# A Gram matrix in a linear-attention encoder layer: one fp32 matmul replaced by three float32r passes over split operands

## The chip, the cores and the metric

The kernel runs on one NeuronCore of a Trainium2 chip. Its engines are TensorE (PE in the profile, with PEld for its weight loads), VectorE (DVE), ScalarE (ACT), GpSimd (POOL) and SyncE (SP), which issues most of the DMAs. Each engine takes its instructions from a queue of its own, in order; semaphores join the engines. The metric is the device time of one execution in microseconds: 1487.59 us in the median of three runs of the kernel before (1486.43 to 1488.28).

## What is computed

One encoder layer on 256 tokens of width 2048, all in float32:

```python
h    = rms_norm(x, norm1_g)
proj = h @ w_in                                  # 2048 -> 11312 columns, split among the mixers
y_m  = mlstm_mixer(m_q, m_k, m_v, m_o, ...)      # 4 heads, two directions
y_d  = gated_deltanet_mixer(d_qkv, d_z, ...)     # 8 heads of 128, two directions, chunks of 64
x = x + (sigmoid(g_m) * (y_m @ w_branch_m) + sigmoid(g_d) * (y_d @ w_branch_d)) @ w_out
x = x + relu(rms_norm(x, norm2_g) @ w_ff1) ** 2 @ w_ff2
return rms_norm(x, norm_f_g)
```

In the DeltaNet mixer each head and direction needs, per stretch of tokens, the products of the keys with the keys and of the keys with the queries, weighted by decays, and a triangular solve with the first of them:

```python
a_mat = where(strict, einsum('id,jd->ij', kb, kc) * gamma, 0) + eye(L)
u = triangular_solve(a_mat, vc * beta);  w = triangular_solve(a_mat, kb * exp(gc))
attn = einsum('id,jd->ij', qc, kc) * gamma
```

The two products, keys with keys and keys with queries, are the Gram matrix that the change is about.

## The kernel before

**The weight stream.** Every large product (projection, branch products, output product, the two feed-forward products) is cut into granules of two 128-row tiles of a weight matrix, up to 512 columns each. For a granule SP loads `raw`, ACT rounds it to float32r (`wh`), DVE subtracts to get the rest (`wl`), and PE does three passes: high weights with high activations, low with high, high with low. Four `wh`/`wl` buffers hold granules that are split three ahead of PE. A granule of 512 columns is 12 matmuls; its results collect in PSUM tiles of the pool `ps_acc`, of which there are four, two to a chunk of a product.

**The mixers beside it.** Everything else is written as tasks (Python generators) that yield the engine they want next. A planner (`_Clocks`, `pick`, `pump`, `force`) keeps an estimated clock for each engine from a table of costs (`cost`, L60) and puts a task's next step into the program between two half granules when its estimated inputs are ready. The order that comes out is fixed in the program. `force` (L251) is used where the stream can't go on until some task has moved: it then puts in the tasks' steps one after another, whatever their time. A granule's matmuls, and what is forced while they are asked for, are put in with `clk.quiet` set (L415), under which `issue` (L94) leaves the clocks as they are.

**The DeltaNet task.** `mixers` runs, in this order, `delta_solve(0)` (heads 0 to 3), the mLSTM, `delta_solve(1)` (heads 4 to 7). One `delta_solve` is a long chain: the Gram matmuls of four heads (`pk`, L1036 to L1043, two to a head, each 128 by 512: the 512 columns of `kq` are 256 tokens of keys and 256 of queries), their weighting by decays into `ba` on DVE, a 32 by 32 inversion on DVE of which the inputs and results go through DRAM (`dpx`, `nblk`, `xblk`, `Rb`), small matmuls that widen the inverse (`pz`, `pp`, into `u`), and then a block solve in two steps, each `pA`, `Y`, `pR`, `vy` or `vx`, `pB`, `Y`, and at last the outputs `po`. `delta_out` scales them (`yd`), sums their squares (`jkd`, `ssd`), takes the root (`rs`, `rd`) and multiplies by the gates.

**The shared slots.** The tag `tmp` has four 512-column buffers. The gate product `z` comes in two chunks that hold two each (`sgz`) from their evacuation until `z_mul` (L829) has used them, which needs `so1`, the end of `delta_out` of the second four heads. The evacuation of a chunk of the merge gates `gm` takes two (`sgm`, L1267), and the branch product `bm` of the same number waits for it. A chunk gives its two PSUM accumulators back after its evacuation only; the next chunk asks for two (`mms` in `gemm`):

```python
                    while left["acc"] < 2:
                        force()
```

The tag `w4` has three buffers, used by the convolution, the gates' rows and the inversion.

Of the kernel before, what the change touches and what calls it, by code (L numbers as in the profile page):

```python
# [9 lines left out]
F32 = mybir.dt.float32  # L10
F32R = mybir.dt.float32r
# [5 lines left out]
P = 128  # L17
# [32 lines left out]
class _Clocks:  # L50
# [9 lines left out]
    def cost(self, e, name, a, k):  # L60
        if name == "dma_start":
            return 1.1 if e == "G" else 0.1
        if e == "T":

            sw, self.slab = 0.3 if self.slab else 0.0, False
            if name == "transpose":
                return 0.11 + sw
            n = a[2].free_size()
            c = 4 * max(n, 128) / 2400
            if "tile_position" in k:  # L70
                c *= max(a[1].free_size(), 32) / 128
            return c + sw
        n = a[0].free_size()
        src = a[1] if len(a) > 1 and hasattr(a[1], "free_size") else None
        ps = src is not None and src.space == PSUM
        if e == "A":
            c = ((61 if ps else 112) + n) / 1200
            if any(hasattr(k.get(x), "free_size") for x in ("scale", "bias")):
                c += 0.093
            if "accum_out" in k:  # L80
                c += 0.19
            f = TABLES.get(a[2]) if name == "activation" else None
            if f and f != self.table:
                self.table = f
                c += 1.3
            return c
        if e == "V":
            if name == "reciprocal":
                return 0.1 + 8 * n / 960
            half = name in ("tensor_copy", "tensor_scalar") and not ps and a[0].space != PSUM  # L90
            return (66 + (n / 2 if half else n)) * 1.042e-3 + (0.06 if "scalar" in name else 0)
        return 0.1 + n * (2.2e-3 if name != "memset" else 0.9e-3)
# [64 lines left out]
def layer_kernel(ctx, tc, x, xt, cst, prm, w_in, w_bm, w_bd, w_out, w_ff1, w_ff2, gf, out):  # L157
    nc = tc.nc
    clk = _Clocks()
    V, A, T, G = (_Ordered(tc, e, k, clk) for e, k in  # L160
                  ((nc.vector, "V"), (nc.scalar, "A"), (nc.tensor, "T"), (nc.gpsimd, "G")))
# [112 lines left out]
    def get(what, n, e):  # L274
        while left[what] < n:
            yield None
        left[what] -= n
        yield e

    def put(what, n):  # L280
        left[what] += n

    def psm(shape, name):
        while not psfree:
            yield None
        clk.cur.ext = max(clk.cur.ext, psfree.pop(0))
        yield "T"
        return ps_m.tile(shape, F32, tag="m", name=name)

    def rel(n=1):  # L290
        psfree.extend([clk.cur.last()] * n)
# [144 lines left out]
    pm = mx.enter_context(tc.tile_pool(name="pm", bufs=1))  # L436
# [586 lines left out]
    def delta_solve(grp):  # L1023
# [8 lines left out]
        kq, bd, rq = D[grp]["kq"], D[grp]["bd"], D[grp]["rq"]  # L1032
        ba = pm.tile([P, 4, 2, 768], F32, tag="ba", name="ba")
        bk = ba[:, :, 0, :].rearrange("p h (b c) -> p h b c", c=128)
        clk.cur.fork()
        for hh in range(4):  # L1036
            clk.cur.fork()
            pks = []
            for s_ in range(2):
                pk = yield from psm([P, 2, 256], "pk")  # L1040
                pks.append(pk)
                T.matmul(pk.rearrange("p a b -> p (a b)"), kq[:, hh, s_ * 128:s_ * 128 + 128], kq[:, hh, :],
                         start=True, stop=True)  # L1043
            for s_, pcs in ((0, ((0, 0, 256, 0), (1, 384, 512, 0))), (1, ((0, 256, 384, 128), (1, 512, 768, 0)))):
                yield "V"
                for d, lo, hi, t0 in pcs:
                    n = hi - lo
                    V.scalar_tensor_tensor(ba[:, hh, :, lo:hi], pks[s_][:, :, t0:t0 + n], bd[:, d, s_, hh:hh + 1],
                                           cm[:, hh, lo:hi].unsqueeze(1).broadcast_to([P, 2, n]),
                                           op0=ALU.mult, op1=ALU.mult)  # L1050
                rel()
# [23 lines left out]
        for r in range(31, 0, -1):  # L1075
            n = 32 - r
# [21 lines left out]
        for d in range(2):  # L1098
            for pp in range(2):
# [3 lines left out]
                for hh in range(4):  # L1103
                    for t in range(2):
                        u = unit(d, hh, t)
                        c = DIAG[d, t] + 32 * b1
# [38 lines left out]
        for stp in range(2):  # L1145
# [3 lines left out]
            else:  # L1149
                vts = []  # L1150
                pxs = []
                for d in range(2):
                    px = yield from psm([P, 4, 128], "px")
                    pxs.append(px)
                    c = 128 if d == 0 else 512
                    for hh in range(4):
                        T.matmul(px[:, hh, :], ba[:, hh, 0, c:c + 128], Y[:, d, 1 - tt_[d], hh, :],
                                 start=True, stop=True)
# [20 lines left out]
            for d in range(2):  # L1179
# [3 lines left out]
                for hh in range(4):  # L1183
                    c = DIAG[d, tt_[d]] + hb.start
# [30 lines left out]
        for t in range(2):  # L1215
# [3 lines left out]
            for hh in range(4):  # L1219
                for i, (d, s_, c) in enumerate(lst):  # L1220
                    T.matmul(po[:, hh, :], ba[:, hh, 1, c:c + 128], Y[:, d, s_, hh, :], start=(i == 0),
                             stop=(i == 2))
# [28 lines left out]
    def mixers():  # L1251
        yield from delta_solve(0)
        yield from mlstm_weights()
        yield from mlstm_heads()
        yield from delta_solve(1)
        ydT[0] = pm.tile([P, 16, S], F32R, tag="ba", name="ydT")
        yield from wait_for("T", "z0", "z512")
        yield from y_T(yd[0], ydT[0][:, 0:8, :], ydT[0][:, 8:16, :], lambda kt: dgc)
        done("ydT")
# [528 lines left out]
```

## Time and profile before

| | |
|---|---|
| runs | 1487.59 us median (1486.43 to 1488.28) |
| the profiled execution's own time | 1486.63 us |
| its span, from the first instruction to the last | 1484.8 us |
| mean granted TensorE clock | 0.998 of full |
| PE busy | 1472.0 us, 99% |
| PEld busy | 1235.2 us, 83% |
| DVE busy | 923.9 us, 62% |
| ACT busy | 770.3 us, 52% |
| share of PE in the chain that ended last | 93% |

A matmul's duration in the profile runs from its start to its modelled end, and neighbours overlap, so what a matmul costs is read from start to start. A matmul in fp32 shows as two recorded instructions, one in float32r as one. "x96" in a row of a view that merges neighbours is 96 recorded instructions one after another. Times of the views count from the start of the span.

### The profile page before, as it was taken

How to read it: one execution, taken by the hardware profiler on the slowest of the kernel's cores; microseconds unless marked ns; L12 is line 12 of the kernel's file. 1: busy time of each engine (PE TensorE's matmuls, PEld its weight loads, DVE VectorE, ACT ScalarE, POOL GpSimd, SP SyncE). 2: the span in 40 equal slices, each digit the busy share in tenths (PEclk: the TensorE clock that was granted, in tenths of full speed). 3: DMA queues.
4: the chain of work that ended last, by engine and by line, in shares of the span. 5: the costliest groups of instructions: out<-in, count | busy, mean ns of one | idle time of the engine just before them, and what ended most of it. 6: DMA issues, size and time to landing. Idle time of an engine off the chain costs nothing.

```text
span 1484.8 us, 20192 instructions
## 1 busy us (share of the span) xinstructions
PE 1472.0 (99%) x7604; PEld 1235.2 (83%) x7604; DVE 923.9 (62%) x1400; ACT 770.3 (52%) x1128; POOL 29.2 (2%) x68
## 2 busy tenths in 40 slices
PE   9999999999999999999999999999999999999997
PEld 8787788888878888888888888888888888888886
DVE  6678784378779546565556565555555555555865
ACT  6686545565765456444544444444344444444664
POOL 0000110000010100000000000000000000000000
PEclk9999999999999999999999999999999999999999
DMA  9665576465667845777656666666666666666664
GB/s 317 205 201 169 171 209 187 149 180 160 182 196 225 245 114 150 217 255 252 201 171 199 188 189 190 185 187 189 191 182 189 196 193 193 196 191 194 186 199 140
DMA packets 147730, 287.01 MB, mean 193 GB/s; under 512 B 9956, under 2 KB 24804, under 8 KB 147632
## 3 DMA queue, kind: packets, MB, share of 16 engines
q1 hardware_dynamic: 145088, 278.78, 62.3%
q0 software_dynamic: 2256, 6.58, 1.3%
q8 instruction: 59, 0.97, 0.3%
q10 hardware_dynamic: 288, 0.37, 0.1%
q14 instruction: 39, 0.32, 0.1%
HBM read 278.32 MB, written 7.36 MB: 192 GB/s over the span
## 4 chain that ended last, share of the span: by engine, by line
PE 93%; DMA 3%; ACT 2%; DVE 1%; issue 1%; SPq 0%; ACTq 0%
PE f L125 24%; PE y L125 23%; PE gd L125 6%; PE gm L125 6%; PE wo L125 6%; PE d L125 5%; PE mv L125 3%; PE bd L125 3%; PE bm L125 3%; DMA raw<-in_w_in_dram 3%; PE z L125 2%; PE mq L125 1%; PE mk L125 1%; PE o L125 1%; PE pk L125 1%; ACT wh L125 1%
## 5 line engine op out<-in xcount | busy, mean ns | idle before, releaser
L125 DVE TENSOR_TENSOR wl<-raw,wh 128x1024 fp32r<-128x1024 f32 (+3 forms) x508 | 603.8, 1193 | 468.9 <-ACT wh L125 467.5
L125 ACT CAST wh<-raw 128x1024 fp32r<-128x1024 f32 (+3 forms) x508 | 520.7, 1028 | 562.1 <-PE y L125 162.4
L125 PE MATMUL f<-h,wh 128*128 128x512 f32 x1024 | 277.3, 394 | 0.1
L125 PEld LDWEIGHTS f<-h,wh 128*128 128x128 f32 x1024 | 176.1, 189 | 25.2 <-DVE x L125 0.7
L125 PE MATMUL y<-wh,ah 128*128 128x512 f32 (+1 forms) x514 | 179.0, 388 | 0.0
L125 PE MATMUL y<-wl,ah 128*128 128x512 f32 (+1 forms) x514 | 178.8, 388 | 0.0
L125 PE MATMUL y<-wh,al 128*128 128x512 f32 (+1 forms) x514 | 178.7, 388 | 0.0
L125 PEld LDWEIGHTS f<-h,wl 128*128 128x128 f32 x1024 | 155.0, 189 | 20.3
L125 PE MATMUL f<-h,wl 128*128 128x256 f32 x1024 | 160.4, 281 | 0.0
L125 PEld LDWEIGHTS y<-wh,ah 128*128 128x128 f32 x514 | 96.5, 188 | 20.2 <-DVE u L125 0.4
L125 PEld LDWEIGHTS y<-wl,ah 128*128 128x128 f32 x514 | 96.5, 188 | 19.9
L125 PEld LDWEIGHTS y<-wh,al 128*128 128x128 f32 x514 | 96.5, 188 | 19.9
L125 PE MATMUL d<-wh,xTh 128*128 128x512 f32 x192 | 77.3, 402 | 0.0
L125 PE MATMUL d<-wl,xTh 128*128 128x512 f32 x192 | 75.1, 391 | 0.0
L125 PE MATMUL d<-wh,xTl 128*128 128x512 f32 x192 | 74.9, 390 | 0.0
L125 PE MATMUL gd<-wh,xTh 128*128 128x512 f32 x128 | 51.0, 398 | 0.0
L125 DVE TENSOR_TENSOR al<-aT,ah 128x256 fp32r<-128x256 f32 x128 | 50.9, 419 | 0.0
L125 PE MATMUL wo<-wh,mTh 128*128 128x512 f32 x128 | 50.5, 394 | 0.0
L125 PE MATMUL gm<-wh,xTh 128*128 128x512 f32 x128 | 50.1, 391 | 0.0
L125 PE MATMUL wo<-wh,mTl 128*128 128x512 f32 x128 | 49.9, 390 | 0.0
L125 PE MATMUL gd<-wl,xTh 128*128 128x512 f32 x128 | 49.9, 390 | 0.0
L125 PE MATMUL wo<-wl,mTh 128*128 128x512 f32 x128 | 49.8, 389 | 0.0
(312 smaller groups left out, 2017.4 us busy)
## 6 DMA issues: line engine op xcount, KB each, us to landing
raw<-in_w_ff_dram SPq DMA_DIRECT2D x256, 512.0 KB, 3.8
raw<-in_w_in_dram SPq DMA_DIRECT2D x160, 512.0 KB, 4.0
raw<-in_w_out_dram SPq DMA_DIRECT2D x32, 512.0 KB, 4.6
raw<-in_w_bm_dram SPq DMA_DIRECT2D x16, 512.0 KB, 4.4
raw<-in_w_bd_dram SPq DMA_DIRECT2D x16, 512.0 KB, 4.3
raw<-in_w_in_dram SPq DMA_DIRECT2D x16, 256.0 KB, 2.8
mx<-dgm SPq DMA_DIRECT2D x16, 256.0 KB, 5.1
cmd<-dcr SPq DMA_DIRECT2D x12, 256.0 KB, 5.4
```

What stands on the lines that cost most here:

```text
L125: return self._tc.keep_in_program_order(f(*a, **k))
```

## The change

The Gram matmul of `kq` in fp32 becomes three float32r passes. For each head ACT rounds the 128 by 512 tile to `kh`, DVE subtracts to `kl`, both in one buffer of the tag `w4`, and PE does high with high, high with low and low with high. The planner's cost table gets a price for a float32r matmul.

```diff
         if e == "T":
 
-            sw, self.slab = 0.3 if self.slab else 0.0, False
+            r = name == "matmul" and a[2].dtype == F32R
+            sw = 0.3 if self.slab and not r else 0.0
+            self.slab = self.slab and r
             if name == "transpose":
                 return 0.11 + sw
             n = a[2].free_size()
+            if r:
+                return n / 2400 + 0.0134
...
         for hh in range(4):
+
             clk.cur.fork()
+            yield from get("w4", 1, "A")
+            khl = pm.tile([P, 2, 512], F32R, tag="w4", name="khl", bufs=3)
+            kh, kl = khl[:, 0, :], khl[:, 1, :]
+            A.copy(kh, kq[:, hh, :])
+            yield "V"
+            V.tensor_sub(kl, kq[:, hh, :], kh.bitcast(F32))
             pks = []
             for s_ in range(2):
                 pk = yield from psm([P, 2, 256], "pk")
                 pks.append(pk)
-                T.matmul(pk.rearrange("p a b -> p (a b)"), kq[:, hh, s_ * 128:s_ * 128 + 128], kq[:, hh, :],
-                         start=True, stop=True)
+                c = slice(s_ * 128, s_ * 128 + 128)
+                o = pk.rearrange("p a b -> p (a b)")
+                T.matmul(o, kh[:, c], kh, start=True, stop=False)
+                T.matmul(o, kh[:, c], kl, start=False, stop=False)
+                T.matmul(o, kl[:, c], kh, start=False, stop=True)
+            put("w4", 1)
```

Because the planner sets the order from its estimates, the instructions of all engines come in another order from the first Gram matmul to the last chunk of the gate products. Three places show it.

On PE at the first Gram matmuls, in the key projection `mk` of the mLSTM, four matmuls of `kqd` (two heads) stood together before:

```order
L125 MATMUL mk_1356<-wh,xTl 128x512
L125 MATMUL pcol<-cs,hs_1284 128x4 x4
L125 MATMUL pk<-kqd 128x512 x4
L125 MATMUL mk_1355<-wh,xTh 128x512
L125 MATMUL mk_1355<-wl,xTh 128x512
```

and now six passes of one head stand there, 12 matmuls of the stream later:

```order
L129 MATMUL mk_1356<-wh,xTl 128x512
L129 MATMUL pcol<-cs,hs_1284 128x4 x4
L129 MATMUL mk_1355<-wh,xTh 128x512
...
L129 MATMUL mk_1356<-wh,xTl 128x512
L129 MATMUL pk<-khl 128x512 x6
L129 MATMUL mk_1355<-wh,xTh 128x512
```

Counted from the first matmul of `mk`, 72 matmuls of the stream stood ahead of the last Gram matmul of the first four heads, and now 150; for the second four heads it moves 156 matmuls of the stream further back, from the middle of the output-gate product `o` into the first `bm` chunk.

On PE at the second step of the block solve for the second four heads (`pA` from `vx`, then `pR`, `pB`, and the outputs `po`) the stream's matmuls stood between the four before; the stretches left out are 24, 24 and 12 matmuls of `z` and `gm`, and 84 of `gm` follow `po`:

```order
L125 MATMUL pA<-vx,u_4536 64x128 x8
L125 MATMUL z_0_4953<-wh,xTh 128x256
...
L125 MATMUL pR<-Y,ba 64x128 x8
...
L125 MATMUL pB<-vx,u_4536 64x128 x8
L125 MATMUL gm_0_5156<-wh,xTh 128x512
...
L125 MATMUL po<-Y,ba 128x128 x24
L125 MATMUL gm_0_5156<-wh,xTh 128x512
```

and now they follow each other, between the last matmul of the branch product `bm` of chunk 2 and the first of the gates `gm` of chunk 3:

```order
L129 MATMUL bm_1_5282<-wh,ymTl 128x512
L129 MATMUL pA<-vx,u_4862 64x128 x8
L129 MATMUL pR<-Y,ba 64x128 x8
L129 MATMUL pB<-vx,u_4862 64x128 x8
L129 MATMUL po<-Y,ba 128x128 x24
L129 MATMUL gm_0_5500<-wh,xTh 128x512
```

The whole end of the chain has moved behind the `z` chunks and behind chunk 2 of `gm` and `bm`, and no matmul of the stream stands between its parts.

On ACT at the same place, after the copies of the first step (`Y` from `pA` and `pB`), casts of the stream stood between the steps, and five of them between the root `rs` and the evacuation `sgm` of a chunk of gates:

```order
L125 COPY Y<-pB 64x512 x2
L125 CAST wh<-raw 128x1024
L125 ACTIVATE jkd,ssd<-yd 128x128 x4
L125 CAST wh<-raw 128x1024
L125 ACTIVATE jkd,ssd<-yd 128x128 x4
L125 CAST wh<-raw 128x1024
L125 ACT_TABLE_LOAD
L125 ACTIVATE rs<-ssd 128x8
L125 CAST wh<-raw 128x1024 x5
L125 ACT_TABLE_LOAD
L125 ACTIVATE sgm<-gm_0_5156,r_79 128x512
```

and now there is none:

```order
L129 COPY Y<-pA 64x512 x2
L129 COPY Y<-pB 64x512 x2
L129 ACTIVATE jkd,ssd<-yd 128x128 x8
L129 ACT_TABLE_LOAD
L129 ACTIVATE rs<-ssd 128x8
L129 ACT_TABLE_LOAD
L129 ACTIVATE sgm<-gm_0_5032,r_79 128x512
L129 ACTIVATE sgm<-gm_1_5033,r_79 128x512
L129 CAST wh<-raw 128x1024
```

`sgm` of chunk 2, `gm_0_5032`, now stands behind `rs` of the second four heads without anything of the stream between; in the queue of DVE the products of `yd` with `zc` (4) and `sgz` (12) stand between `rd` and the use of `sgm`.

## Rows read from the trace of the kernel before

**Rows 1.** First block of the page: engine, busy us, share of the span, instructions.

```profile
PE 1472.0 (99%) x7604; PEld 1235.2 (83%) x7604; DVE 923.9 (62%) x1400; ACT 770.3 (52%) x1128; POOL 29.2 (2%) x68
```

**Rows 2.** What PE waited for: us in total, times, longest us.

```profile
PE zp L449 <- DVE zw L446: 1.5, 1, 1.5
PE o L125 <- DVE wl L125: 1.1, 2, 0.6
```

**Rows 3.** Timeline of PE: start, us, instruction, count; then the chain of waits.

```profile
425.78 3.60 PE L125 MATMUL pk<-kqd 128*128 128x512 f32 x8
...
429.44 0.39 PE L125 MATMUL o<-wl,xTh 128*128 128x512 f32 x1
...
475.62 21.76 PE gm L125 x96
```

**Rows 4.** Instruction groups by form: splits of 512 columns (count, busy us, mean ns, idle).

```profile
L125 DVE TENSOR_TENSOR wl<-raw,wh 128x512 fp32r<-128x512 f32 x16 | 10.9, 689 | 12.5 <-ACT wh L125 12.5
L125 ACT CAST wh<-raw 128x512 fp32r<-128x512 f32 x16 | 9.8, 618 | 9.0 <-PE z L125 5.5 <-PE gd L125 2.7 <-DMA raw<-in_w_in_dram 0.6
```

**Rows 5.** Timeline of PE, block solve of the second four heads, 546 to 566 us.

```profile
546.85 1.58 PE L125 MATMUL pA<-vx,u 64*64 64x128 f32 x16
...
555.99 1.58 PE L125 MATMUL pB<-vx,u 64*64 64x128 f32 x16
...
557.83 0.40 PE L125 MATMUL gm<-wl,xTh 128*128 128x512 f32 x1
...
560.35 5.52 PE L125 MATMUL po<-Y,ba 128*128 128x128 f32 x48
...
565.94 0.40 PE L125 MATMUL gm<-wl,xTh 128*128 128x512 f32 x1
```

**Rows 6.** Timeline of ACT, the same stretch and the evacuation after it, 547 to 585 us.

```profile
547.98 1.19 ACT L125 COPY Y<-pA 64x512 f32<-64x512 f32 x2 [1.83 <-PE pA L125]
...
566.69 0.31 ACT L125 ACTIVATE jkd<-yd 128x128 f32<-128x128 f32 x1
...
568.21 0.19 ACT L125 ACTIVATION_READ_ACCUMULATOR jkd<-yd 128x1 f32 x1
...
569.71 1.28 ACT L125 ACT_TABLE_LOAD   x1
571.00 0.21 ACT L125 ACTIVATE rs<-ssd 128x8 f32<-128x8 f32 x1
...
584.61 0.69 ACT L125 ACTIVATE sgm<-gm,r 128x512 f32<-128x512 f32 x1
```

**Rows 7.** Timeline of DVE, the same stretch, 552 to 581 us.

```profile
552.54 1.40 DVE L125 TENSOR_TENSOR vx<-vx,pR 64x512 f32<-64x512 f32 x2
...
565.90 0.69 DVE L125 TENSOR_TENSOR yd<-po,ssr 128x512 f32<-128x512 f32 x1 [1.99 <-PE po L125]
...
572.30 1.14 DVE L125 SCALAR_TENSOR_TENSOR yd<-yd,rd,zc 128x128 f32<-128x128 f32 x4
...
576.31 2.18 DVE L125 SCALAR_TENSOR_TENSOR yd<-yd,rd,sgz 128x128 f32<-128x128 f32 x8
...
579.54 1.14 DVE L125 SCALAR_TENSOR_TENSOR yd<-yd,rd,sgz 128x128 f32<-128x128 f32 x4
```

**Rows 8.** Windows: length, busy of PE, PEld, DVE, ACT, POOL, granted clock, DMA.

```profile
1476.00:1477.00 1.00, 0.18 (x2) 0.00 (x0) 0.79 (x2) 0.27 (x1) 0.00 (x0) 1.00 1.06 406
...
1478.00:1479.00 1.00, 0.00 (x0) 0.00 (x0) 0.76 (x5) 0.13 (x2) 0.00 (x0) 1.00 0.00 0
1479.00:1480.00 1.00, 0.00 (x0) 0.00 (x0) 1.00 (x2) 1.00 (x2) 0.00 (x0) 0.51 0.00 0
```

**Rows 9.** Timeline of PE, the start of the program.

```profile
1.46 3.69 PE L449 MATMUL zp<-zw 128*128 128x128 f32 x18 [1.46 <-DVE zw L446]
```

**Rows 10.** Windows, as in rows 8, around the first Gram matmuls.

```profile
140.00:200.00 60.00, 60.00 (x265) 46.92 (x264) 51.41 (x96) 28.69 (x38) 4.35 (x8) 1.00 0.59 171
```

## The prediction

> **What bounds the kernel now.** I read the page's busy shares first: PE is busy for 1472.0 of 1484.8 us, everything else at most 83% [rows 1]. Then the waits of PE alone: the longest are 1.5 us for its first operand and 1.1 us for a `wl` [rows 2], so PE hardly ever stands still. The chain of waits says the same (93% PE). So two things change the time: work taken off PE, which counts in full, and any place where PE now has to wait, which counts in full too, since behind such a place there is no idle time that could take it up. After that I read the timeline of PE, ACT and DVE at the places where the order changed.
>
> **What the Gram matmuls save.** In the second four heads eight halves, that is four fp32 matmuls, run from 425.78 to the stream's second matmul behind them at 429.44 [rows 3]. The stream's pace is 21.76 us for 96 matmuls, 0.227 us each [rows 3]; one of those lies in that stretch, so four Gram matmuls cost 3.66 - 0.227 = 3.43 us, 0.86 each (start to start; the 0.59 us that a record lasts is no cost). There are 16, in five such blocks: 13.7 us. The new 48 passes have the stream's shape and type and cost 48 x 0.227 = 10.9 us. The saving is **2.8 us**, all of it on PE. A pass could be no slower than the stream's, and no row shows a faster one; for the block ends I keep 2.4 to 3.2.
>
> **What the split adds.** Eight casts on ACT and eight subtractions on DVE of 512 columns, 0.62 and 0.69 us each [rows 4], 5.0 and 5.5 us in all. Between the passes of one head and those of the next the new order has 12 to 36 matmuls of the stream, 2.7 to 8.2 us, and the split of the next head lies beside them; DVE is the tighter engine there (51.4 of 60 us busy around the first Gram matmuls [rows 10]). I take nothing, with 0 to 12 us as the bounds (the upper one is a rival below).
>
> **What the new order adds.** The Gram matmuls wait for the split and for a `w4` buffer, so they spread over more granules, and the whole chain of the mixers shifts back, for the second four heads by 156 matmuls of the stream (35 us). Before, the last product of that chain ended at 579.54 + 1.14 = 580.7, and the evacuation of `gm` chunk 2 came at 584.61 [rows 6, 7]: it had four microseconds to spare. With the shift the two `z` chunks hold all four `tmp` buffers when `gm` chunk 2 wants two, so it keeps its accumulators, `bm` chunk 2 waits for it and keeps the other two, and `gm` chunk 3 has none. The planner then forces the rest of the chain in, and does so inside `mms`, with its clocks held: it doesn't see that this takes time. So PE meets `pA`, `pR`, `pB`, `po` and the first `gm` of chunk 3 with nothing between them, and each waits for ACT or DVE.
>
> I add up that chain from the start of `pA` (time 0), with durations of before. A step has two halves, one per direction. `pA` starts at 546.85 and the first copy at 547.98: 1.13 us from a half's start to its evacuation; two copies take 1.19 [rows 5, 6], two subtractions 1.40 [rows 7]. With 0.1 us from an evacuation to PE (my estimate from the gaps between such rows):
> - second copy of `pA` ends at 2.3; second half of `pR` at 2.4, its subtraction from 3.65 (behind the first half's) to 4.35; second half of `pB` at 4.45, its copy from 5.6 to 6.2; `po` at 6.25. If the halves didn't overlap it would be 7.3.
> - `po` start to the end of the second `yd`: 560.35 to 566.59, 6.24 us [rows 5, 7]: 12.5.
> - its squares `jkd`, 566.69 to 568.40 [rows 6], 1.71 us and a gap of 0.1: 14.3. The table load and the root, 569.71 to 571.21 [rows 6]: 15.8. Then five small steps until the first `yd` with `zc` at 572.30 [rows 7], 1.09 us: 16.9.
> - four products with `zc` (1.14) and eight with `sgz` of the first `z` chunk (2.18) [rows 7]. `sgm` of `gm` chunk 2 takes the buffers of that chunk: the first after four of the eight, the second after all, at 20.2; it lasts 0.69 [rows 6], so both accumulators are free at about 21.0.
>
> In that time PE does useful work: 1.61 us for each of `pA`, `pR`, `pB` (555.99 to 557.83 less one stream matmul) and 5.36 us for `po` (560.35 to 565.94 less one) [rows 5], 10.2 us in all, and 0.7 us of `gm` when the first accumulator is free. The new idle time is 21.0 - 10.2 - 0.7 = **10.1 us**. From below: ACT's own order puts `sgm` behind the root, so even with all products free it can't end before 15.8 + 1.28 + 2 x 0.69 = 18.5, which leaves 7.6 us. From above: no overlap of halves (+1.05) and all twelve products with `sgz` first: 13.6 us. What follows is provided for: the stream is split three granules (8 us) ahead, and ACT and DVE go back to splitting one or two microseconds after PE starts again.
>
> **The clock.** [...] In the new place PE has 8 us without work, from the end of `po` (11.8) to the first accumulator (19.9). [...] What that costs I take from the start of the program: 18 halves of a 128 by 128 fp32 matmul take 3.69 us there, 0.205 each [rows 9], and 48 halves of the same shape in `po` 5.52 us, 0.115 each [rows 5]; 18 x 0.09 = **1.6 us** until the engine was at full speed. Bounds: 0 and twice that.
> [...]
>
> **The sum.** -2.8 + 10.1 + 1.6 = +8.9 us on the profiled execution's own 1486.63: 1495.5. The median of the runs lies 0.96 above that execution, so I expect **1496.5 us**. Its own range, from the bounds: -3.2 + 7.6 + 0 = +4.4 and -2.4 + 13.6 + 3.2 = +14.4, 1492 to 1502.
>
> **Rivals.**
> - *The accumulators are free after all (not slower).* If `gm` chunk 3 got two accumulators that nobody holds, its first granules would run while the chain ends, and only the gaps between `pA` and `po` stayed: 6.25 - 4.83 = 1.4 us, all told -2.8 + 1.4 = -1.4: 1486.2. It decides as soon as chunk 3 starts before `sgm` of chunk 2. For it: an order shows no waits. Against it: four accumulators, two held by `gm` and two by `bm` of chunk 2, and the stream left out of the order just there. Chance 0.06.
> - *The split is late as well.* If every head's passes waited for its cast and subtraction (0.62 + 0.69 + two hops of 0.1, eight times), 12 us would be added: 1508.5. For it: DVE's share [rows 10], and that DVE takes its queue in order. Against it: the matmuls of the stream between. If half of the heads waited, it would be 1502. Chance 0.07.
> - *The clock falls earlier.* If the gaps between `pA`, `pR` and `pB` were enough to bring it down, `po` would run at half pace, 5.4 us more, and lengthen the chain by as much: 1502. [...] Against it from rows: PE works for 4.8 of those 6.25 us. Chance 0.12.
>
> **How the numbers follow.** My forecast has 0.75. A difference under 0.2%, 3 us, can't be told from no change. Faster by more comes only if the first rival holds and the wait is smaller still: 0.03; within 0.2%: 0.04; slower: 0.93. The range for 8 in 10 leaves out the first rival and the far end of the second: 1491 to 1503.
>
> **What would show it.** Right: the 16 Gram matmuls as 48 single records at 0.227 us; PE waiting for `Y`, `vx` and `yd`, and then some 8 us for `sgm`, between the last `bm` of chunk 2 and `gm` of chunk 3; the window behind it at a granted clock of 0.5; the same pace before and behind. Wrong: `gm` of chunk 3 starting before `sgm` of chunk 2, waits of PE for `khl`, or any lasting gain or loss elsewhere.

## The result, and the profile after

The changed kernel takes 1502.09 us in the median of four runs (1500.63 to 1504.22), the kernel before 1487.16 us beside it: a ratio of 1.0099 (95% interval 1.0086 to 1.0112), **slower by 14.9 us**. The forecast was slower by 8.9 us, 1496.5, range 1491 to 1503. The direction, the place and the wait were right; a term of four to five microseconds was missing.

The profiled run has an own time of 1504.22 us and a span of 1502.3. The first line of its page answers to [rows 1]: PE is busy 4.8 us longer, the span is 17.5 us longer, so the loss is mostly PE waiting.

```profile
PE 1476.8 (98%) x7620; PEld 1244.0 (83%) x7620; DVE 929.1 (62%) x1408; ACT 769.8 (51%) x1133; POOL 29.2 (2%) x68
```

What PE waited for, the four longest entries and one further down (us in total, times, longest us), beside [rows 2]:

```profile
PE gm L129 <- ACT sgm L129: 8.1, 1, 8.1
PE gm L129 <- ACT wh L129: 2.3, 1, 2.3
PE ptd L129 <- ACT tmd L129: 1.9, 1, 1.9
PE zp L453 <- DVE zw L450: 1.5, 1, 1.5
...
PE gm L129 <- DVE wl L129: 0.8, 1, 0.8
```

The 8.1 us for `sgm` are the forecast wait. The waits of `gm` for `wh` and `wl`, 3.1 us, were not in the forecast. No row says that PE waited for `khl`.

**The wait before `gm` chunk 3.** The timeline of PE there (start, us, instruction, count, idle before it and what ended that), which answers to [rows 5]:

```profile
591.62 1.58 PE L129 MATMUL pA<-vx,u 64*64 64x128 f32 x16
593.37 1.69 PE L129 MATMUL pR<-Y,ba 64*64 64x128 f32 x16 [0.17 <-ACT Y L129]
595.24 1.79 PE L129 MATMUL pB<-vx,u 64*64 64x128 f32 x16 [0.18 <-DVE vx L129]
596.96 0.49 PE L129 MATMUL po<-Y,ba 128*128 128x128 f32 x2
597.70 5.40 PE L129 MATMUL po<-Y,ba 128*128 128x128 f32 x46 [0.25 <-ACT Y L129]
611.19 0.80 PE L129 MATMUL gm<-wh,xTh 128*128 128x512 f32 x1 [8.09 <-ACT sgm L129]
```

And the chain that it waits for, on ACT:

```profile
605.64 1.28 ACT L129 ACT_TABLE_LOAD   x1
606.94 0.21 ACT L129 ACTIVATE rs<-ssd 128x8 f32<-128x8 f32 x1
...
610.45 0.69 ACT L129 ACTIVATE sgm<-gm,r 128x512 f32<-128x512 f32 x1 [2.00 <-DVE yd L129]
611.50 0.69 ACT L129 ACTIVATE sgm<-gm,r 128x512 f32<-128x512 f32 x1 [0.36 <-DVE yd L129]
```

Counted from `pA` (591.62), the forecast put `po` at 6.25, the end of the root at 15.8, the first accumulator at 19.9 and the second at 21.0. They came at 6.08, 15.5, 19.57 and 20.57. The rows on PE follow each other without a matmul of the stream between them, so every gap in them is lost.

**The clock behind it.** Windows of the same stretch (length, busy of PE, PEld, DVE, ACT, POOL, granted clock, DMA):

```profile
606.00:608.00 2.00, 0.00 (x0) 0.00 (x0) 0.71 (x4) 1.97 (x3) 0.00 (x0) 0.96 0.00 0
608.00:610.00 2.00, 0.00 (x0) 0.00 (x0) 1.94 (x8) 0.45 (x1) 0.00 (x0) 0.50 0.00 0
...
612.00:614.00 2.00, 2.00 (x6) 1.51 (x6) 2.00 (x5) 1.12 (x2) 0.58 (x1) 0.50 0.00 0
614.00:616.00 2.00, 2.00 (x10) 1.62 (x9) 0.85 (x1) 0.00 (x0) 0.55 (x1) 0.83 0.66 254
```

The engine had no work from about 603.1, its granted clock fell from 1.00 to 0.50 near 607.9, and `gm` chunk 3 ran at half pace, 0.43 us from matmul to matmul, until about 614.7. So a wait in the middle of the program is followed by a slow start here: 8.1 us of wait, and then half pace. From the last `bm` to behind the slow stretch, wait and clock lost 11.2 us: of the 26.1 us from 591.53 to 617.65, 14.9 are work at full pace (10.2 for `pA` to `po`, 13 matmuls of `gm` at 0.227, and 1.75 for `pty`, as in the kernel before). Forecast were 10.1 + 1.6 = 11.7.

**What was not forecast: `gm` chunk 2.** Timeline of PE at the end of the second `z` chunk (256 columns wide) and the start of `gm` chunk 2:

```profile
542.30 0.28 PE L129 MATMUL z<-wh,xTl 128*128 128x256 f32 x1
544.87 0.50 PE L129 MATMUL gm<-wh,xTh 128*128 128x512 f32 x1 [2.29 <-ACT wh L129]
546.13 0.58 PE L129 MATMUL gm<-wl,xTh 128*128 128x512 f32 x1 [0.76 <-DVE wl L129]
546.51 0.63 PE L129 MATMUL gm<-wh,xTl 128*128 128x512 f32 x1
546.93 0.63 PE L129 MATMUL gm<-wh,xTh 128*128 128x512 f32 x1
```

The cast that PE waits for, on ACT, had itself waited for its load:

```profile
543.77 1.04 ACT L129 CAST wh<-raw 128x1024 fp32r<-128x1024 f32 x1 [4.34 <-DMA raw<-in_w_in_dram]
```

The weights are late, PE stands still, and the clock falls here too: the last rows are 0.42 us apart instead of 0.227, and the granted clock is 0.50 from 547 to 549. Before the change the short granules had the solve's matmuls between them (`pA` of [rows 5] among them); those have moved away, and the granules follow each other every 1.44 us. The loss here is worked out once the experiments have given its parts.

### The profile page after: what moved, and what is told of

It reads as the page before. It is cut to its first block, busy times and chain, and to the rows that moved or that the text cites. A ratio compares the mean times of both kernels' runs of the same rounds, so it can differ in the third digit from the quotient of the medians.

```text
span 1502.3 us, 20234 instructions
## 1 busy us (share of the span) xinstructions
PE 1476.8 (98%) x7620; PEld 1244.0 (83%) x7620; DVE 929.1 (62%) x1408; ACT 769.8 (51%) x1133; POOL 29.2 (2%) x68
## 4 chain that ended last, share of the span: by engine, by line
PE 93%; DMA 3%; DVE 2%; ACT 1%; issue 0%; SPq 0%; ACTq 0%
PE f L129 24%; PE y L129 23%; PE d L129 7%; PE gm L129 6%; PE gd L129 6%; PE wo L129 6%; PE bm L129 3%; PE mv L129 3%; PE bd L129 3%; DMA raw<-in_w_in_dram 3%; PE o L129 2%; PE mq L129 1%; PE mk L129 1%; PE z L129 1%; DVE wl L129 1%; PE oif L129 1%
## 5 line engine op out<-in xcount | busy, mean ns | idle before, releaser
L129 PE MATMUL gm<-wl,xTh 128*128 128x512 f32 x128 | 51.2, 400 | 0.8 <-DVE wl L129 0.8
L129 PE MATMUL gm<-wh,xTl 128*128 128x512 f32 x128 | 51.1, 399 | 0.0
```

What stands on the lines that cost most here:

```text
L129: return self._tc.keep_in_program_order(f(*a, **k))
```

## The experiments

Theories: (A) the wait before chunk 3 comes from the four `tmp` buffers, through the accumulators; (B) the late weights come from the run of short granules; both come from the new order. Rivals: the loss is in the passes or in the split; the late weights are chance or a collision.

**b_order: the passes in the old order.** The order of the kernel before is kept on every engine; only splits and passes are added. `split` does the cast to `kh` and the subtraction to `kl` of one head.

```diff
+        split(0)
+        split(1)
...
-                T.matmul(pk.rearrange("p a b -> p (a b)"), kq[:, hh, s_ * 128:s_ * 128 + 128], kq[:, hh, :],
-                         start=True, stop=True)
...
+                T.matmul(o, kh[:, c], kh, start=True, stop=False)
...
+                T.matmul(o, kh[:, c], kl, start=False, stop=False)
+                T.matmul(o, kl[:, c], kh, start=False, stop=True)
...
+            if hh < 2:
+                split(hh + 2)
```

> The order of the kernel before is kept on every engine; only the split of each head (cast on ACT, subtraction on DVE, two heads ahead of its use) and the three float32r passes stand where the fp32 Gram matmuls stood. Theory (the arithmetic itself gains 2.8 us and the whole loss is of the order): 2.8 us faster than the kernel before, about 1484.4, with the 48 passes at 0.227 us and no wait of PE for the split. Rival (the split is dear): four splits a block crowd ACT and DVE, PE waits for a wl or for kl, and the time is at or above that of the kernel before, by up to 12 us. Rival (the loss lies in the arithmetic): slower by about 15 us as the changed kernel is.

Measured: 1495.2 us (1494.16 to 1497.87), ratio 1.006 (1.0047 to 1.0073). My theory for it fell: in the old places the three passes lose 8 us. PE's waits:

```profile
PE pk L125 <- DVE ba L125: 3.6, 3, 2.1
PE pq L125 <- ACT cacc L125: 2.0, 2, 1.6
PE ptq L125 <- ACT tmq L125: 2.0, 1, 2.0
```

The longest of them, on PE, on DVE and on ACT:

```profile
433.03 0.47 PE L125 MATMUL pk<-kh 128*128 128x512 f32 x1 [2.13 <-DVE ba L125]
```

```profile
431.13 0.69 DVE L125 TENSOR_TENSOR kl<-kqd,kh 128x512 fp32r<-128x512 f32 x1 [1.47 <-ACT kh L125]
431.74 2.19 DVE L125 SCALAR_TENSOR_TENSOR ba<-pk,bd,cmd 128x512 f32<-128x512 f32 x4
```

```profile
428.24 1.28 ACT L125 ACT_TABLE_LOAD   x1
429.54 1.06 ACT L125 ACTIVATE cp<-cacc 128x1024 f32<-128x1024 f32 x1
430.50 1.12 ACT L125 CAST kh<-kqd 128x512 fp32r<-128x512 f32 x2
```

`kh` of the next heads stands behind a table load and a sigmoid of the convolution on ACT, `kl` waits for it, `ba` stands behind `kl` on DVE, and only `ba` frees the PSUM tiles for the next passes. So with the gain of 2.6 us that a_fp32 below shows, the split and what hangs on it cost an estimated 10.7 us there (8.1 + 2.6), which is the late-split rival, in the old order. The profile has 7.6 us of it as the waits above, and the granted clock below 1.00 from 166.3 to 169.8, behind the 2.0 us wait of `ptq` (0.997 in the mean of the profile). My own placing of the split (in front of the weighting) has a part in it, and how much wasn't tried. It also says that the order of the changed kernel, which spreads the heads, is what hides the split.

**a_zmid: the second `z` chunk behind `bm` chunk 2.**

```diff
-              "o0 o1 gm0 bm0 gm1 bm1 z0 z1 gm2 bm2 gm3 bm3").split():
+              "o0 o1 gm0 bm0 gm1 bm1 z0 gm2 bm2 z1 gm3 bm3").split():
```

> The changed kernel with its second z chunk moved from before gm chunk 2 to behind bm chunk 2 (gm2 bm2 z1 gm3 bm3). Then gm chunk 2 finds two free tmp buffers and is evacuated at once, and the solve chain of the second four heads stands between matmuls of the stream again. Theory: both losses of the changed kernel go, the wait between bm 2 and gm 3 (11.4 us with the slow clock behind it) and the late weights at gm chunk 2 (5 us); 1484.5 to 1486.5. Rival 1, that only the wait goes and a bare 256-column chunk costs 3 to 5 us wherever it stands: 1488 to 1490 (here the chunk has pA, pR and pB between its granules, so this would be surprising). Rival 2, that the loss lies in the Gram passes or the split: unchanged, 1499 to 1502.

Measured: 1486.53 us (1485.1 to 1487.35), ratio 0.9995 (0.9987 to 1.0004). Both losses are gone at once, as the theory has it; no wait for `sgm`, `wh` or `wl` is left in PE's list. The time lies at the edge of the forecast range: against the kernel before only 0.6 us are gained, and the interval (1.9 us faster to 0.6 slower) does not reach the 2.6 us of the passes. Where the rest went is not shown.

**a_sigc: the second `z` chunk's sigmoids in another tag.** This takes away the shortage of `tmp` alone and leaves the chunk order.

```diff
-            yield from get("tmp", 2, "A")
...
+            if c0:
...
+                sz = pm.tile([P, 2, 256], F32, tag="sigc", name="sgz1")
...
+            else:
+                yield from get("tmp", 2, "A")
...
```

> The changed kernel with the same chunk order, but the sigmoids of the second z chunk lie in a buffer of another tag (sigc), so two tmp buffers are left for gm chunk 2. Theory (the wait comes from the four tmp buffers, through the accumulators): gm chunk 3 starts without waiting for the end of the solve chain, 11.4 us less than the changed kernel, about 1490; the late weights at gm chunk 2 (some 5 us, PE waiting for wh and wl after the bare 256-column z chunk) stay and show as waits of PE. Rival (the order of the chain alone makes the wait, whoever holds the buffers): still 8 us of PE waiting for sgm or yd, 1499 to 1502.

Measured: 1489.85 us (1486.05 to 1491.52), ratio 1.0018 (1.0008 to 1.0027), 12.2 us below the changed kernel. Of PE's waits the one for `sgm` is gone and those for the weights remain:

```profile
PE gm L129 <- ACT wh L129: 3.2, 1, 3.2
PE zp L453 <- DVE zw L450: 1.5, 1, 1.5
PE o L129 <- DVE wl L129: 0.6, 2, 0.4
PE gm L129 <- DVE wl L129: 0.5, 1, 0.5
```

That shows theory A: with two more buffers, the planner has `gm` matmuls to put between the steps of the solve again (4.5 us from `pA` to `pR` instead of 1.75). The ten runs lie up to 5.5 us apart, so the size of the loss that remains varies from one execution to the next, and in the fastest of them little of it can be left. But the waits are no accident of one profile: all six with the short `z` chunk bare and in small granules (after, after2, a_sigc, a_zswap, a_warm, a_fp32) have waits for `wh` and `wl`, 1.9 to 3.7 us, where it ends or just behind.

**a_zswap: the short `z` chunk first.**

```diff
-              "o0 o1 gm0 bm0 gm1 bm1 z0 z1 gm2 bm2 gm3 bm3").split():
+              "o0 o1 gm0 bm0 gm1 bm1 z1 z0 gm2 bm2 gm3 bm3").split():
```

> The changed kernel with its two z chunks in the other order, the one of 256 columns first, so that it stands away from the loads of the inverse (Rb) that fell beside it. The wait before gm chunk 3 stays. Theory A (twelve short granules in a row use up the lead of the weights wherever they stand, and the clock falls): the loss of 5 us moves to the start of the other z chunk, time as the changed kernel, 1500 to 1502. Theory B (the short granules collide with the loads of the inverse): PE waits only about 1 us there, as at the short chunk of o, and the time is 3 to 5 us less, 1496 to 1498.

Measured: 1500.22 us (1499.09 to 1502.92), ratio 1.0087 (1.0071 to 1.0102): the loss has moved with the chunk (which has eight granules, not twelve). PE waits 2.4 us for `wh` and `wl` of `z`, and the windows where the wide `z` chunk begins (columns as above) show the gap and the clock:

```profile
520.00:522.00 2.00, 0.77 (x4) 0.25 (x2) 0.96 (x1) 1.76 (x2) 0.00 (x0) 1.00 0.78 263
522.00:524.00 2.00, 1.68 (x4) 1.33 (x5) 1.49 (x2) 1.08 (x2) 0.00 (x0) 0.63 0.36 87
524.00:526.00 2.00, 2.00 (x6) 1.57 (x5) 1.72 (x3) 1.25 (x4) 0.00 (x0) 0.52 0.93 284
```

The loads of the inverse (`Rb`) are not there; stores and loads of the gates (`dgm`, `mx`) are. So the loss comes without `Rb` too, though a collision as such is not excluded by this run.

**a_sigc4: the short chunk in longer granules.** The kernel of a_sigc, with the same bytes and the same matmuls, but four 128-row tiles to a granule.

```diff
+        m = 4 if name == "z512" else 2
...
-                for kk in range(2):
+                for kk in range(m):
...
-        for g in range(0, kt, 2):
+        for g in range(0, kt, m):
```

> The kernel of a_sigc with one thing more: the second z chunk (256 columns) is cut into 4 granules of four 128-row tiles instead of 8 of two, so that each load and each split is as large as that of a 512-column granule and stands 2.9 us of PE ahead of the next instead of 1.44. Theory (three raw buffers are three granules of lead; behind short granules that is 4.3 us, and a 512-column granule needs 4.9 us for its load and 1.04 and 1.23 for cast and subtraction, 7.2 us): the wait of about 3 us at the first matmul of gm chunk 2 and the slow clock behind it go, 3 to 5 us less than a_sigc, 1485 to 1487, and PE shows no wait for wh there. Rival (the DMA engines are at their limit there, or other transfers are in the way): the bytes are the same, the wait stays within 1 us, and the time is that of a_sigc, 1489 to 1491.

Measured: 1486.62 us (1484.3 to 1488.48), ratio 0.9988 (0.9979 to 0.9997), 3.2 us below a_sigc by the medians, 4.5 by the two ratios. No wait for `wh` or `wl` of `gm`, the two `z` chunks last 33.27 us instead of 36.66, and the stream goes on without a gap:

```profile
538.74 0.28 PE L129 MATMUL z<-wh,xTl 128*128 128x256 f32 x1
538.86 0.40 PE L129 MATMUL gm<-wh,xTh 128*128 128x512 f32 x1
539.10 0.40 PE L129 MATMUL gm<-wl,xTh 128*128 128x512 f32 x1
```

That shows the condition that theory B names: with the same bytes and the same matmuls in longer granules the loss is gone. The DMA rows of the changed kernel from 525 to 556 us (count, KB, median us from issue to landing) give an estimate of why:

```profile
raw<-in_w_in_dram SPq DMA_DIRECT2D x8, 512.0 KB, 4.9
raw<-in_w_in_dram SPq DMA_DIRECT2D x6, 256.0 KB, 3.2
```

Three raw buffers are three granules of lead. Behind granules of 1.44 us that is 4.3 us, and a large granule needs 4.9 + 1.04 + 1.23 = 7.2 us from the issue of its load to the end of its split: 2.9 us too few, where 3.1 us of waits were seen. With granules of 2.88 us the lead is 8.6 us.

That the two agree so well is partly luck. In the trace the first load of `gm` chunk 2 is issued at 537.25, 5.2 us before the `z` chunk ends at 542.42, and it takes 6.15 us to land. The three loads at this place, in the changed kernel (537.2 to 540.5 us) and in a_sigc4 (532 to 536 us):

```profile
raw<-in_w_in_dram SPq DMA_DIRECT2D x3, 512.0 KB, 6.2
raw<-in_w_in_dram SPq DMA_DIRECT2D x3, 512.0 KB, 4.9
```

So the lead was longer than the estimate and the load slower than the median. How much of the loss is the short lead and how much the slower loads is not shown: a_sigc4 changes both. In a_zswap, away from the `Rb` loads, the loads at the corresponding place took 5.2 us. Nor was the inversion on DVE taken away alone. It stands beside the splits of the short chunk in both orders and delays subtractions that free `raw`: in the changed kernel one cast ends at 526.12 and its subtraction begins at 528.86.

**a_zmid4: a_zmid with both short chunks in long granules,** that of `o` too. The granules are cut as in a_sigc4, on another condition; the line of a_sigc4 and the one here:

```diff
-        m = 4 if name == "z512" else 2
+        m = 4 if cw == 256 else 2
```

> The kernel of a_zmid with both 256-column chunks (o and z) in granules of four 128-row tiles. Theory: the wait of some 1 us for wl at the short chunk of o goes as well, 0 to 1.5 us less than a_zmid, 1485 to 1486.5; against the kernel before -1 to -2.5 us. Rival: the larger granules come later (a longer first load) and move the order, so that something else waits: above 1487.

Measured: 1483.7 us (1482.93 to 1486.2), ratio 0.9976 (0.9965 to 0.9987): faster than both kernels, 4 us below the one before in the same comparison, and 1.3 us below the range that was forecast for it.

**b_gran4: the same granules in the kernel before,** with its fp32 Gram matmuls; the edit is that of a_zmid4.

> The kernel before, Gram matmuls in fp32, with both 256-column chunks in granules of four 128-row tiles, as in a_zmid4. Theory (granules give back some 1 us at the short chunk of o, and the rest of the lead of a_zmid4 is the 2.8 us of the Gram passes): 1486 to 1487.5, within 1.2 us of the kernel before and 2 to 3.5 us above a_zmid4. Rival (all of that lead is the granules'): 1483.5 to 1484.5.

Measured: 1486.15 us (1485.21 to 1489.56), ratio 0.9998 (0.9989 to 1.0007). So the lead of a_zmid4 is not the granules' alone: the passes, together with an order that doesn't wait, are worth some 3 us (0.9998 - 0.9976 = 0.0022). That is near the 2.6 us of the passes, but the two kernels differ in the order too, and these runs don't separate the two.

**a_warm: work for PE in the wait.**

```diff
...
+            for _ in range(32):
+                T.matmul(zp[:, 0:128], ident, ident, start=True, stop=True)
...
```

> The changed kernel with 32 products of the identity with itself (128 by 128, fp32, the result unused) on PE behind po of the second four heads, which fill most of the wait for sgm. Theory (the wait brings the clock down, and the first 3.4 us of gm chunk 3 run at half pace): granted clock 1.00 there, pitch 0.227 us from the first matmul, 1.6 to 1.9 us less than the changed kernel, about 1499. Rival (the slow start of gm chunk 3 has another cause, such as late weights): unchanged, within 0.5 us of 1501.

Measured: 1500.27 us (1500.05 to 1503.48), ratio 1.0088 (1.0074 to 1.0101). The times alone don't tell the theories apart, the trace does. On PE:

```profile
600.06 7.31 PE L129 MATMUL zp<-cs 128*128 128x128 f32 x64
608.32 0.50 PE L129 MATMUL gm<-wh,xTh 128*128 128x512 f32 x1 [0.94 <-ACT sgm L129]
608.65 0.39 PE L129 MATMUL gm<-wl,xTh 128*128 128x512 f32 x1
608.88 0.40 PE L129 MATMUL gm<-wh,xTl 128*128 128x512 f32 x1
```

`gm` chunk 3 starts as late behind `pA` as without it (19.58 us, and 19.57), the granted clock stays at 1.00, the pace is full from the first matmul, and the stretch from there to `bm` chunk 3 lasts 24.04 us instead of 25.32 (25.60 in after2). The slow clock is worth 1.3 us, and 1.6 in after2; 1.6 were forecast.

**a_fp32: the new order with fp32 Gram matmuls.**

```diff
-                T.matmul(o, kh[:, c], kh, start=True, stop=False)
-                T.matmul(o, kh[:, c], kl, start=False, stop=False)
-                T.matmul(o, kl[:, c], kh, start=False, stop=True)
...
+                T.matmul(o, kq[:, hh, c], kq[:, hh, :], start=True, stop=True)
...
```

The lines left out give the planner the price of the three passes, so that the order stays.

> The changed kernel in its own order, with the split kept, but with one fp32 matmul for each Gram tile in place of the three passes (the split parts are written and not read). Theory (the passes gain 2.8 us whatever the order): 2.8 us more than the changed kernel, 1503 to 1505. Rival (a pass costs as much as an fp32 half here, or the gain is hidden behind other waits): unchanged, 1500.5 to 1502.

Measured: 1503.44 us (1502.29 to 1505.87), ratio 1.0101 (1.0086 to 1.0117). By the times it can't be told from the changed kernel, whose interval it overlaps. By the traces the stretch from `mk` to `gd`, with the first eight Gram tiles, is 1.32 us longer than in the changed kernel, and the stretch from `gm` chunk 0 to `gm` chunk 1, with the last eight, 1.28 us: the passes save 2.6 us. In this profile the granted clock stayed at 1.00 at `gm` chunk 2, in spite of 2.0 and 0.8 us of waits, and from the start of that chunk to that of `bm` chunk 2 it took 28.65 us, and 30.25 in the changed kernel: 1.6 us is the price of the slow clock there.

**before2 and after2: both kernels once more.**

> The kernel before once more, for a second profile of it. Theory (the 3.1 us that the profiled run of the changed kernel had lost before the first Gram matmul belong to the execution and not to the kernel, since the order is the same there): the start of mk varies among profiles of the kernel before too, between 129.5 and 132.6 us. Rival (it belongs to the changed program): 129.5 within 0.3 us.

> The changed kernel once more, for a second profile. Theory: the wait for sgm before gm chunk 3 (8.1 us) and the late weights at gm chunk 2 (2 to 4 us of waits) come again, the loss before mk (3.1 us) only by chance; 1500.5 to 1504.5. Rival (the late weights are chance): no wait of PE for wh or wl at gm chunk 2, and a time of 1498 or less.

Measured: 1486.56 and 1500.84 us. `mk` starts at 130.59 and 130.44 us; in the first profiles it was 129.48 and 132.58. So the 3.1 us that the first profile of the changed kernel had lost by then were its own chance: a wait of `ptd` for `tmd` near 50 us, which is there in the kernel before too (1.6 us in before2), and after which the granted clock fell to 0.50 in that one profile (52 to 54 us). after2 has the other losses again: 8.1 us for `sgm`, 1.1 and 0.8 us for `wh` and `wl` (just under the 2 to 4 us that were expected), the slow clock behind both (0.50 from 544 to 546 and from 608 to 610).

## Why the prediction was right, and what it missed

| term | forecast, us | measured, us | from |
|---|---|---|---|
| Gram passes | -2.8 | -2.6 | a_fp32 |
| split | 0 | 0 | no wait for `khl` |
| wait before `gm` chunk 3 | +10.1 | +9.9 | 11.2 less the clock |
| slow clock behind it | +1.6 | +1.3 to +1.6 | a_warm, against the first profile and after2 |
| late weights at `gm` chunk 2, with their clock | none | +3.9 to +5.2 | after2 and the first profile |
| sum | +8.9 | +12.8 to +13.8 | |

The late weights are, for after2 and the first profile: the two `z` chunks last 34.52 and 35.89 us, 33.27 where nothing waits (a_sigc4); the second matmul of `gm` comes 1.26 us behind the first instead of 0.23; and the slow clock takes 1.6. That is 1.25 + 1.03 + 1.6 and 2.62 + 1.03 + 1.6.

From the start of `mk` to that of `bm` chunk 3 the two profiles of the changed kernel take 503.93 and 502.73 us, those of the kernel before 489.70 and 488.58, so they are 13.0 to 15.4 us apart. The rest up to 14.9 is of the size of what varies from one execution to the next: waits at the short chunk of `o`, and the start.

The measured 1502.09 us lies in the forecast range, near its end of 1503. That is luck: that end was made of halves that don't overlap, of all products first, of twice the clock and of a late split, none of which came. The missing term only fitted in.

- **What bounds the kernel**: right. Behind `gm` chunk 3 the difference to the kernel before stays the same to the end of the program; nothing takes it up.
- **The Gram matmuls**: right. Six passes take from 453.49 to 454.88, 1.39 us for 128 by 512 twice, 0.23 each.
- **The split at no cost**: right for this order, by the work that was named. b_order shows that the upper bound was no idle one: without the spread it costs about that.
- **The new order**: right in mechanism and size. a_sigc shows the link by `tmp`, which the prediction read from the order; a_zmid undoes all of it.
- **The clock**: right, with 1.3 to 1.6 us where 1.6 were forecast. That 1.6 was an estimate: no row of the kernel before shows a fall behind a wait, only the one to 0.51 behind the last matmul [rows 8], and at the start, from which the 1.6 is taken, the granted clock is 1.00 in every window from 0 to 6 us although the 18 halves of [rows 9] take 0.205 us each. What the runs showed in its place is the fall to 0.50 behind 8.1 us of wait, and the 1.3 to 1.6 us that a_warm saves behind it. The rival of the earlier fall didn't come: the 46 `po` records took 5.40 us at a granted clock of 1.00.
- **The step that failed** is the sentence "What follows is provided for: the stream is split three granules (8 us) ahead". It was worked out for 512-column granules and for the place behind the wait. When the solve's steps move away, they also leave the place where they were, and there they had stretched the 256-column granules, whose three are 4.3 us. The prediction costed what a moved step meets in its new place, and not what it uncovers in the old one: it put that at nothing, and it was 3.9 to 5.2 us. Of its own signs of being wrong, "any lasting gain or loss elsewhere", this is one. A row that bears on it stood in the profile: the wait for `wl` at the short chunk of `o`, 1.1 us [rows 2], the one other place with bare short granules.

Open is why PE waits only 0.3 to 1.1 us for `wl` at the short chunk of `o` in the two kernels, where the granules are as short; it wasn't tried alone. In a_zmid no wait is left there with short granules either, and with long ones none in a_zmid4 or b_gran4. A part of it may be the loads: the first of 512 KB behind that chunk took 3.7 us from issue to landing in the kernel before and 3.3 in before2, against 6.2 at `gm` chunk 2 in the changed kernel and 5.6 in after2. What made these slower is not shown.

## What to carry to other kernels

A step that a planner moves is costed at both ends: what waits for it where it goes, and whose cover it was where it stood. A lead that is counted in granules is a lead in time only as long as the granules last as long; at a change from short to long granules it has to cover load and split of the long one. A cheaper operation is worth its saving only in an order that has no new wait in it: here the same passes gave +14.9, +8 and -4 us, by the order, the place of the split and the granules.

## What the runs showed of the hardware

- The granted clock also fell in the middle of the program, to 0.50, and sometimes behind short waits: at `gm` chunk 2 with 1.1 and 0.8 us of waits (after2), at `ptd` with 1.9 us in the first profile of the changed kernel; it stayed at 1.00 with 1.4 to 1.9 us at `ptd` in others (after2, before2, a_zmid4, a_fp32), and with 2.0 and 0.8 us at `gm` chunk 2 in a_fp32. The length of the wait alone didn't decide it there.
- At `gm` chunk 2 the fall came after the work had begun again: in after2 PE starts `gm` chunk 2 at 541.23, and the half pace, 0.43 us from matmul to matmul, begins near 543.5 and lasts until 546.9.
- With 7.31 us of the wait filled by matmuls whose result nobody uses, the granted clock stayed at 1.00 and `gm` chunk 3 started no later (19.58 us behind `pA`, and 19.57); that gave back 1.3 us of the 11.2 (a_warm).
